# A transformer layer on one core: attention with its gate chunks and branch B in an order fixed by the text on all engines, tanh gates, and bias and mask summed behind the first FFN's down product

## The chip, the cores and the metric

The kernel runs on one core of a Trainium2 chip. A core has TensorE (PE: matmuls and transposes, results in PSUM banks of 128 x 512 floats), VectorE (DVE), ScalarE (ACT), GpSimd (POOL) and SyncE (SP, which here only starts DMAs; POOL starts some too). Each of them has a queue of its own. The metric is the device time of one execution in microseconds (us); less is better.

## The reference

One layer of an encoder, in float32, for 1024 tokens of width 1024:

```python
h = h + 0.5 * swiglu(rms_norm(h), w_gate, w_up, w_down)             # first FFN, 2816 wide
u = rms_norm(h)
qa, ka, va, qb, kb, vb, ga, gb = split(u @ w_in)
ya = neighbourhood_attention_2d(qa, ka, va, na_rpb)                 # branch A: 8 heads, relative bias and mask
yb = windowed_gqa_sink(rope(qb), rope(kb), vb, sink_logit)          # branch B: 8 heads on 2 kv heads, window, sink
merged = sigmoid(ga) * (ya @ w_branch_a) + sigmoid(gb) * (yb @ w_branch_b)
h = h + merged @ w_out
h = h + 0.5 * swiglu(rms_norm(h), ...)                              # second FFN
y = rms_norm(h)
```

Heads are 64 wide. In both attentions a block of 128 queries sees at most its own block of keys and its two neighbours.

## The kernel before

**Products.** Float32 operands are split into a high part (a copy on ACT in float32r) and a residual (source minus high part, DVE): `split`, L92 to L94. `mm3` (L142 to L149) makes a product of three matmuls for two banks: high times high, high times low, low times high. In each, the first operand is loaded as weights and serves both banks. Large products run by Strassen's scheme with seven sub-products P1 to P7 (`products`, L234; `Down`, L503). `Down.run` takes 77 steps for the FFN's down product (seven sub-products by 11 blocks of 128) and at each step calls the functions that are filed under its number in `loads`.

**Stages.** First FFN, hidden part and down product; the mixer's projection (five groups of four of the 34 column blocks of `w_in` that it needs); attention; branch products; output projection; second FFN. The other 14 column blocks are gate columns. They are not computed with the projection but as filling in attention (`gate`, L1132): a gate is a 128 x 1024 block, made in 48 matmuls of 128 x 512 into two PSUM banks; then ACT copies the banks out (L1143), and a DMA on POOL's queue stores them. Its weight is loaded as 128 x 1024 and split by one ACT cast (L93) and one DVE residual (L94).

**Attention** is 64 units, one for two heads and 128 queries: 32 of branch B (0 to 31), then 32 of branch A (32 to 63). Three steps, each a unit behind the one before: `scores` (L1284): for each head two matmuls of up to 128 x 384 (L1294, L1295), one DVE operation that adds bias or mask and finds the row's extreme (L1299), and the exp on ACT with its row sum (L1302); then reciprocal (L1305) and scaling, one head on DVE (L1306), one on ACT (L1307). `turn` (L1309): six transposes (L1315), with a split of each head (L93 on ACT, L94 on DVE). `values` (L1322): six matmuls (L1329 or L1334), a copy on ACT (L1247, L1268), and adds on DVE (L1249; L1269 and L1272). In the loop (L1352 to L1379) a turn has the scores of unit n, filling, the transposes of unit n - 1, filling, the values of unit n - 2. I call these the unit's first and second filling. Filling comes from the generator `filler` (L1215): the gates, then the products of branch B (`branch_b`, L1198) and of branch A.

**PSUM.** There are eight banks in two groups of four, g and d. Scores and transposes take d. Values and gates take g, a gate two banks at a time.

**Order.** Before, the text hands instructions to a scheduler, which decides each engine's order. Sigmoid opens the gates (L1195, L1409). The sum of bias and mask is made in `load_bias` (L1085 to L1091), two heads at a time, within attention.

## Time and profile before

| | |
|---|---|
| time, median of three runs | 1931.56 us (1931.3 to 1931.82) |
| the profiled execution | 1931.21 us, span 1929.4 us, clock 0.999 |
| busy: PE, DVE, ACT, POOL | 1919.3, 1434.0, 944.2, 296.1 us |
| first FFN: hidden part, down product | 0 to 413, 413 to 655 us |
| mixer's projection | 655 to 839 us |
| attention with gates | 839 to 1118 us |
| first branch products | 1118 to 1200 us |

A line of the profile's timeline has start, duration, engine, line, operation, and output<-input. Matmuls overlap and their ends are modelled, so a chain of them is read from start to start. A row of `order`, below, has the line, the operation, output<-input with the tiles' numbers, and the shape; [waits ...] names the engines whose semaphores the instruction waits for.

### The profile page before, as it was taken

The page shows a single profiled execution, that of the slowest core. Times are in us where ns is not written, and L with a number is a line of the kernel's source. Part 1 is how long each engine was busy: PE and PEld are TensorE (multiplying, and loading weights), DVE is VectorE, ACT ScalarE, POOL GpSimd, SP SyncE. Part 2 cuts the span into 40 slices and gives each one's busy share as a digit, 9 for nine tenths or more (in the row PEclk, how much of TensorE's full clock was granted, in tenths as well). Part 3 has the DMA queues.
Part 4 walks back from the last instruction along what each step waited for, and adds up shares of the span by engine and source line. Part 5 has one row for each costly group of instructions (what it writes and reads, how often), then busy time and mean ns, then how long its engine had stood idle before and what let it go on. Part 6 is the DMA issues. An engine that isn't in the chain of part 4 may idle for free.

```text
span 1929.4 us, 25478 instructions
## 1 busy us (share of the span) xinstructions
PE 1919.3 (99%) x8956; PEld 1602.7 (83%) x8956; DVE 1434.0 (74%) x2560; ACT 944.2 (49%) x1826; POOL 296.1 (15%) x432
## 2 busy tenths in 40 slices
PE   9999999999999999999999999999999999999998
PEld 8888888888888888888888888888888888888886
DVE  8987765668957778678888856889676566569864
ACT  7532333344446543477777862365333333344453
POOL 0011100013300112211122231010111001005210
PEclk9999999999999999999999999999999999999999
DMA  6244323285334467753459676443422322493341
GB/s 267 95 167 166 138 100 125 87 298 215 92 106 138 158 202 240 218 166 102 116 130 195 188 240 212 170 153 121 147 98 103 127 87 106 145 340 114 115 142 61
DMA packets 151745, 298.70 MB, mean 155 GB/s; under 512 B 14912, under 2 KB 64448, under 8 KB 151616
## 3 DMA queue, kind: packets, MB, share of 16 engines
q1 hardware_dynamic: 123072, 210.53, 33.3%
q0 software_dynamic: 27824, 85.48, 13.3%
q8 instruction: 71, 1.16, 0.2%
q10 hardware_dynamic: 720, 1.05, 0.1%
q14 instruction: 58, 0.48, 0.1%
HBM read 210.50 MB, written 88.27 MB: 155 GB/s over the span
## 4 chain that ended last, share of the span: by engine, by line
PE 96%; DVE 2%; ACT 1%; DMA 0%; issue 0%; POOLq 0%; POOL 0%; DVEq 0%
PE g L145 18%; PE g L147 18%; PE g L149 18%; PE d L149 12%; PE d L145 12%; PE d L147 12%; PE d L1315 2%; PE g L1329 1%; PE d L1294 1%; PE d L1295 1%; PE g L1334 1%; PE d L138 1%; DVE ar L94 0%; DMA ahead<-in_w_in_dram 0%; DMA n1c<-in_ffn_norm_dram 0%
## 5 line engine op out<-in xcount | busy, mean ns | idle before, releaser
L145 PE MATMUL g<-ar,ws 128*128 128x512 f32 x1128 | 422.6, 395 | 0.3 <-DVE fa L602 0.3
L147 PE MATMUL g<-ar,ws 128*128 128x512 f32 x1128 | 416.7, 390 | 0.0
L149 PE MATMUL g<-ar,ws 128*128 128x512 f32 x1128 | 416.3, 390 | 0.0
L145 PE MATMUL d<-ar,ws 128*128 128x512 f32 x736 | 281.9, 390 | 0.5 <-ACT ws L309 0.5
L147 PE MATMUL d<-ar,ws 128*128 128x512 f32 x736 | 281.4, 389 | 0.1
L149 PE MATMUL d<-ar,ws 128*128 128x512 f32 x736 | 281.2, 389 | 0.1
L149 PEld LDWEIGHTS g<-ar,ws 128*128 128x128 f32 x1128 | 211.7, 188 | 44.8
L147 PEld LDWEIGHTS g<-ar,ws 128*128 128x128 f32 x1128 | 211.8, 188 | 44.6
L145 PEld LDWEIGHTS g<-ar,ws 128*128 128x128 f32 x1128 | 206.4, 188 | 36.4 <-issue 0.7
L312 DVE TENSOR_TENSOR ws<-raw,ws 128x512 fp32r<-128x512 f32 x204 | 139.3, 689 | 98.9 <-ACT ws L309 97.9
L309 ACT CAST ws<-raw 128x512 fp32r<-128x512 f32 x204 | 125.0, 620 | 142.2 <-PE g L149 63.8
L145 PEld LDWEIGHTS d<-ar,ws 128*128 128x128 f32 x736 | 138.1, 188 | 29.4 <-ACT ws L309 0.9
L147 PEld LDWEIGHTS d<-ar,ws 128*128 128x128 f32 x736 | 138.1, 188 | 29.3 <-DVE ar L814 0.5
L149 PEld LDWEIGHTS d<-ar,ws 128*128 128x128 f32 x736 | 138.1, 188 | 29.1 <-DVE ws L312 0.5
L93 ACT CAST ws<-raw 128x512 fp32r<-128x512 f32 (+1 forms) x121 | 81.0, 669 | 144.7 <-PE d L149 66.7
L94 DVE TENSOR_TENSOR ws<-raw,ws 128x512 fp32r<-128x512 f32 (+1 forms) x119 | 94.0, 792 | 60.7 <-ACT ws L93 60.5
L415 POOL DMA_DIRECT2D hid<-fx x91 | 49.3, 542 | 432.3 <-DVE fx L475 288.6
L93 ACT CAST ar<-raw 128x512 fp32r<-128x512 f32 (+1 forms) x83 | 56.0, 679 | 93.7 <-PE g L147 55.0
L94 DVE TENSOR_TENSOR ws<-ar,ws 128x512 fp32r<-128x512 f32 x114 | 98.2, 866 | 4.0 <-ACT ws L93 3.9
L145 PE MATMUL g<-ws,ws 128*128 128x512 f32 x232 | 90.9, 392 | 0.0
L149 PE MATMUL g<-ws,ws 128*128 128x512 f32 x232 | 90.4, 390 | 0.0
L147 PE MATMUL g<-ws,ws 128*128 128x512 f32 x232 | 90.3, 389 | 0.0
(313 smaller groups left out, 3604.8 us busy)
## 6 DMA issues: line engine op xcount, KB each, us to landing
raw<-hid SPq DMA_DIRECT2D x70, 512.0 KB
hid<-fx POOLq DMA_DIRECT2D x91, 256.0 KB, 2.3
ar<-in_ffn_w_down_dram SPq DMA_DIRECT2D x32, 512.0 KB
raw<-in_ffn_w_up_dram SPq DMA_DIRECT2D x31, 512.0 KB
raw<-in_ffn_w_gate_dram SPq DMA_DIRECT2D x27, 512.0 KB
raw<-in_w_in_dram SPq DMA_DIRECT2D x27, 512.0 KB
hid<-fa POOLq DMA_DIRECT2D x51, 256.0 KB, 2.6
ar<-zs_d POOLq DMA_DIRECT2D x48, 256.0 KB, 5.0
```

The source lines that it names most:

```text
L93: nc.scalar.copy(dst_hi, src)
L94: (eng or nc.vector).tensor_tensor(dst_lo, src, f32v(dst_hi), op=ALU.subtract)
L138: nc.tensor.transpose(pt[:, c * P:(c + 1) * P], xs[:, (half * 4 + c) * P:(half * 4 + c + 1) * P], ident)
L145: nc.tensor.matmul(b, lhs[0], r[0], start=first, stop=False, **kw)
L147: nc.tensor.matmul(b, lhs[0], r[1], start=False, stop=False, **kw)
L149: nc.tensor.matmul(b, lhs[1], r[0], start=False, stop=last, **kw)
L309: nc.scalar.copy(w[0][:, :512], a)
L312: nc.vector.tensor_tensor(w[0][:, 512:], a, f32v(w[0][:, :512]), op=ALU.subtract)
L415: nc.gpsimd.dma_start(hid[PRODUCTS.index(p), i], src)
L1294: nc.tensor.matmul(b[:, :nw], un["q"][s], un["kd"][s][:, k0 * P:k1 * P], start=True, stop=False)
L1295: nc.tensor.matmul(b[:, :nw], un["q"][s], un["kl"][s][:, k0 * P:k1 * P], start=False, stop=True)
L1315: nc.tensor.transpose(pt[:, i * P:(i + 1) * P], un["pr"][s][:, i * P:(i + 1) * P], ident)
```

## The change

Attention runs in a manual schedule: each engine's queue follows the text. The text is rearranged for it. A unit's `scaled` comes behind the transposes of the unit before, so reciprocal and scaling stand behind that unit's casts and residuals. `values` returns the rest of its `write` as a generator, and DVE's add of the values' halves comes behind the scores of the next unit. `mm3_halves` lets a step of six matmuls be cut into two of three; a gate is 16 such steps, one and two a filling on even units, two and two on odd ones, so that a gate takes 4.57 units. Its weight is split five steps of six before its end, about a unit ahead of the next gate (in units 3, 8, 12, 17 and so on), as one cast of 128 x 1024 and one residual. The copies of the old gate stand where the filling generator reaches them. Gates end in units 4, 9, 13, 18, 22, 27, 31, 36, 41, 45, 50, 54, 59 and 63. The sinks of two heads are copied in one instruction; in branch B one 64 x 256 add replaces two of 64 x 128.

Sums of bias and mask are made in the first FFN's down product: in three calls for each of the eight heads, at steps 2, 5 and 10 plus six times the head's number, a load, two DVE adds, and two stores on SP's queue to `bm_d`. Attention loads the sums into six held tiles. Gates become tanh(x/2) + 1, multiplied in one fused DVE instruction, with the output projection's scale 0.5 in place of 1. Two of the mixer's early weight loads go to tiles that are free sooner, and are issued at the transition's first steps. The splits of y on POOL become splits on DVE, in units 59, 60 and 62 and in the last gate and branch B. The program has as many matmuls as before.

ACT around the end of a gate. Before: `xs_785` is the gate's copy, `g_733` and `g_734` its banks, `ws_765` the next gate's weight.

```order
L93 CAST ws_765_6870<-raw_767_6872 128x1024
L1307 ACTIVATE fa_73<-fa_73,rc_758_6834 128x384
L1247 COPY s1_692_6541<-g_768_6882 64x256
L1302 ACTIVATE fa_73,ssum_771_6894<-fa_73,nmx_770_6893 128x385 x2
L93 CAST ws_775_6917<-d_777_6919 128x3x128
L1307 ACTIVATE fa_73<-fa_73,rc_772_6895 128x384
L93 CAST ws_775_6917<-d_778_6925 128x3x128
L1143 COPY xs_785_6965<-g_733_6719 128x512
L1247 COPY s1_692_6541<-g_779_6937 64x256
L1143 COPY xs_785_6965<-g_734_6720 128x512
```

After, in units 12 and 13: `xs_859` is the copy, `g_809` and `g_810` the banks, `ws_847` the next weight.

```order
L1412 ACTIVATE fa_73<-fa_73,rc_840_7194 128x384
L98 CAST ws_847_7230<-raw_815_7076 128x1024
L1345 COPY s1_699_6593<-g_849_7237 64x256
L1402 ACTIVATE fa_73,ssum_851_7246<-fa_73,nmx_850_7245 128x385 x2
L98 CAST ws_855_7266<-d_857_7268 128x3x128
L98 CAST ws_855_7266<-d_858_7274 128x3x128
L1412 ACTIVATE fa_73<-fa_73,rc_852_7247 128x384
L1204 COPY xs_859_7286<-g_809_7051 128x512
L1204 COPY xs_859_7286<-g_810_7052 128x512
L1345 COPY s1_699_6593<-g_862_7295 64x256
```

The first copy stood behind the second cast of its unit, one copy of values after it; now both stand together, behind both casts and the scaling.

PE at the same two places. Before: the old gate's last matmuls, values (L1334), scores (L1294), then the new gate `g_786`, `g_787`.

```order
L149 MATMUL g_733_6719<-ar_439_4446,ws_710_6623 128x512
L149 MATMUL g_734_6720<-ar_76_589,ws_710_6623 128x512
L1334 MATMUL g_779_6937<-ws_761_6856,fx_649_6140 128x256
L1334 MATMUL g_779_6937<-ws_762_6857,fx_649_6140 128x256
...
L1294 MATMUL d_783_6950<-ar_478_4810,ar_479_4811 128x384 [waits DVE_49]
L1295 MATMUL d_783_6950<-ar_478_4810,ar_479_4811 128x384
L1294 MATMUL d_784_6956<-ar_478_4810,ar_479_4811 128x384 [waits DVE_49]
L1295 MATMUL d_784_6956<-ar_478_4810,ar_479_4811 128x384
L145 MATMUL g_786_6969<-ar_440_4447,ws_765_6870 128x512 [waits Activation_49]
L145 MATMUL g_787_6970<-ar_480_4812,ws_765_6870 128x512 [waits Activation_49]
```

After, unit 13 and the start of 14: the old gate's last three, the new gate `g_860`, `g_861`, values (L1439), scores (L1396).

```order
L162 MATMUL g_810_7052<-ar_76_590,ws_796_6991 128x512
L162 MATMUL g_809_7051<-ar_445_4495,ws_797_6992 128x512
L162 MATMUL g_810_7052<-ar_76_590,ws_797_6992 128x512
L162 MATMUL g_860_7290<-ar_446_4496,ws_847_7230 128x512 [waits Activation_49]
L162 MATMUL g_861_7291<-ar_493_4875,ws_847_7230 128x512 [waits DVE_49]
L162 MATMUL g_860_7290<-ar_446_4496,ws_847_7230 128x512
L1439 MATMUL g_862_7295<-ws_843_7210,fx_659_6195 128x256 [waits Activation_49]
L1439 MATMUL g_862_7295<-ws_844_7211,fx_659_6195 128x256
...
L1396 MATMUL d_866_7307<-ar_491_4873,ar_492_4874 128x384
L1397 MATMUL d_866_7307<-ar_491_4873,ar_492_4874 128x384
```

Before, the new gate began ten matmuls behind the old one's last. Now it follows at once, and the value product that waits for ACT comes three matmuls behind the old gate's last.

DVE at the weight's residual. Before: reciprocal, sink copy, scaling, the residual `ws_766`, the values' adds, then the reductions of the next unit (L1299).

```order
L1305 RECIPROCAL rc_758_6834<-ssum_757_6833 128x2
L1298 COPY fa_73<-nsk_5307 128x1
L1306 TENSOR_SCALAR fa_73<-fa_73,rc_758_6834 128x384
L94 TENSOR_TENSOR ws_766_6871<-raw_767_6872,ws_765_6870 128x1024
L1249 TENSOR_TENSOR xs_769_6889<-g_768_6882,s1_692_6541 64x128 x2
L1299 ISA fa_73,nmx_770_6893<-d_773_6896,masks_548_5302,nsk_5307 128x384
L1299 ISA nmx_770_6893 128x1
L1299 ISA fa_73,nmx_770_6893<-d_774_6902,masks_548_5302,nsk_5307 128x384
L1299 ISA nmx_770_6893 128x1
```

After, from unit 12's reciprocal to unit 13's residuals: `ws_848` is the weight's residual.

```order
L1410 RECIPROCAL rc_840_7194<-ssum_839_7193 128x2
L1411 TENSOR_SCALAR fa_73<-fa_73,rc_840_7194 128x384
L101 TENSOR_TENSOR ws_848_7231<-raw_815_7076,ws_847_7230 128x1024
L1393 COPY fa_73<-nsk_5361 128x2
L1399 ISA fa_73,nmx_850_7245<-d_853_7249,masks_557_5357,nsk_5361 128x384
L1399 ISA nmx_850_7245 128x1
L1399 ISA fa_73,nmx_850_7245<-d_854_7254,masks_557_5357,nsk_5361 128x384
L1399 ISA nmx_850_7245 128x1
L1347 TENSOR_TENSOR xs_827_7138<-g_849_7237,s1_699_6593 64x256
L101 TENSOR_TENSOR ws_856_7267<-d_857_7268,ws_855_7266 128x3x128
```

The residual stands ahead of the next unit's reductions in both; the add came before the reductions and comes now behind them, and the reciprocal is now behind the unit's own two residuals.

The core of the diff:

```diff
+    def mm3_halves(banks, first, last, lhs, rhs):
+
+        parts = [(w, b, r[k], k) for w, k in ((0, 0), (0, 1), (1, 0)) for b, r in zip(banks, rhs)]
+        for i, (w, b, r, k) in enumerate(parts):
+            nc.tensor.matmul(b, lhs[w], r, start=first and w + k == 0, stop=last and w == 1)
+            if i == 2:
+                yield
...
+                if i in early_rooms or (i, m) in early_rooms:
+                    ahead[i, m] = [main.tile([P, 512], F32, tag="hs", bufs=6, name=nm_("ahead")) for _ in range(2)]
+                    for k, r in enumerate(ahead[i, m]):
+                        nc.sync.dma_start(r.rearrange("p (c f) -> p c f", f=P), src(i, m, 0)[:, 4 * k:4 * k + 4])
+                else:
+                    ahead[i, m] = main.tile([P, 1024], F32, tag="ws", bufs=8, name=nm_("ahead"))
+                    fetch(ahead[i, m], i, m, 0)
...
+    bm_d = dram.tile([8, 2, P, 384], F32, name="bm_d")
+    biased = {}
+
+    def hs6():
+        return [main.tile([P, 512], F32, tag="hs", bufs=6, name=nm_("hs"))[:, :384] for _ in range(6)]
+
+    def bias_fetch(h):
+        if h == 0:
+            biased[0] = hs6()
+            for e in range(2):
+                nc.sync.dma_start(biased[0][e], c_mask_a[e])
+        nc.sync.dma_start(biased[0][2 + h % 2], bias_d[h])
+
+    def bias_add(h):
+        for e in range(2):
+            o = biased[0][4 + e]
+            pin(nc.vector.tensor_tensor(o.rearrange("p (d r w) -> p d r w", d=3, r=ROWS),
+                                        biased[0][2 + h % 2].rearrange("p (r d w) -> p d r w", d=3, w=8),
+                                        biased[0][e].rearrange("p (d r w) -> p d r w", d=3, r=ROWS), op=ALU.add))
+
+    def bias_put(h):
+        for e in range(2):
+            nc.sync.dma_start(bm_d[h, e], biased[0][4 + e])
+
+    for h in range(8):
+        for e, f in ((2, bias_fetch), (5, bias_add), (10, bias_put)):
+            k = e + 6 * h
+            down.loads.setdefault(k, []).insert(0, lambda d, f=f, h=h: f(h))
...
+    def gate_split(late=False):
+        h, l, r = ws4(), ws4(), mix["gate"]
+        split(h, l, r, None, late)
+        mix["gate"] = [a.rearrange("p (c f) -> p c f", f=P) for a in (h, l)]
...
-            mm3(bs, k == 0, k == NC8 - 1, (w[0][:, c, :], w[1][:, c, :]), [u_half(c, n) for n in range(2)])
-            yield
+            yield from mm3_halves(bs, k == 0, k == NC8 - 1, (w[0][:, c, :], w[1][:, c, :]), [u_half(c, n) for n in range(2)])
+            if k < NC8 - 1:
+                yield
             if k in steps:
...
+    def open_gate(dc):
+        r = mix["rb", dc]
+        pin(nc.scalar.activation(r, r, AF.Tanh, scale=0.5))
...
-                nc.vector.tensor_tensor(merged(dc)[:, sl], bs[n], rb[:, sl], op=ALU.mult)
+                nc.vector.scalar_tensor_tensor(out=merged(dc)[:, sl], in0=rb[:, sl], scalar=1.0, in1=bs[n],
+                                               op0=ALU.add, op1=ALU.mult)
...
-                yield from gate(dc, {4: lambda: mix.update(gate=load_w(win[0], GA + nxt * P))})
+                yield from gate(dc, {0: lambda: gate_fetch(nxt, raw4()), 5: gate_split})
             else:
-                yield from gate(dc, {0: lambda: [fetch_y(c * P) for c in range(2)],
-                                     4: lambda: [split_y(Y_B[c], c * P, nc.gpsimd) for c in range(2)],
-                                     5: lambda: [fetch_y(c * P) for c in range(2, 4)]})
+                yield from gate(dc, {0: lambda: [fetch_w(0), fetch_w(1)] + [fetch_y(c * P) for c in range(2)],
+                                     2: lambda: fetch_gate(0),
+                                     4: lambda: [split_y(Y_B[0], 0, nc.vector), fetch_y(2 * P)],
+                                     5: lambda: split_w(0),
+                                     6: lambda: [split_y(Y_B[1], P, nc.vector), fetch_y(3 * P)]})
...
                     nc.scalar.copy(lo, o[HD:])
+                    yield
-                    for s in range(2):
-                        nc.vector.tensor_tensor(ybox["b"][s * HD:s * HD + HD, c, :], o[:HD, s, :], lo[:, s, :], op=ALU.add)
+                    yield
+                    nc.vector.tensor_tensor(ybox["b"][:, c], o[:HD], lo, op=ALU.add)
...
+        un["sums"] = ssum, rc
+
+    def scaled(un):
+
+        ssum, rc = un["sums"]
         nc.vector.reciprocal(rc, ssum)
         nc.vector.tensor_scalar_mul(un["pr"][0], un["pr"][0], rc[:, 0:1])
         nc.scalar.activation(un["pr"][1], un["pr"][1], AF.Copy, scale=rc[:, 1:2])
...
-        un["write"](o)
+        rest = un["write"](o)
+        next(rest)
+        return rest
...
-    rate = (nfill - 44) / 64.0
-    spent = 3.0
-
-    def filling(share):
+    n_b = 64
+    spent = 0.0
+
+    def filling(n):
         nonlocal spent
-        spent += rate * share
+        spent += len(gates) * 8 / n_b if n < n_b else 2
         drain(fill, int(spent))
         spent -= int(spent)
...
-    for n in range(1 << 30):
-        got = next(source, None)
-        if got is not None:
-            scores(got)
-        pipe.insert(0, got)
-        for hp, n0 in preps.items():
-            if n == n0:
-                prep = prep_a(hp)
-        if prep:
-            drain(prep, 1)
-        filling(0.5)
-        if len(pipe) > 1 and pipe[1] is not None:
-            turn(pipe[1])
-        if prep:
-            drain(prep, 1)
-        if n in (58, 59, 61):
-            fetch_y(512 + min(n - 58, 2) * P)
-        if n in (60, 61, 62):
-            split_y(Y_A[n - 60], 512 + (n - 60) * P, nc.gpsimd)
-        filling(0.5)
-        if len(pipe) > 2 and pipe[2] is not None:
-            values(pipe[2])
-        pipe = pipe[:3]
-        if not any(pipe):
-            break
-    drain(fill)
+    def attention():
+
+        nonlocal pipe, prep
+        rest = iter(())
+        for n in range(1 << 30):
+            got = next(source, None)
+            if got is not None:
+                scores(got)
+            drain(rest)
+            pipe.insert(0, got)
+            for hp, n0 in preps.items():
+                if n == n0:
+                    prep = prep_a(hp)
+            if prep:
+                drain(prep, 1)
+            filling(n)
+            if len(pipe) > 1 and pipe[1] is not None:
+                turn(pipe[1])
+            if got is not None:
+                scaled(got)
+            if prep:
+                drain(prep, 1)
+            if n >= 26 and (n - 26) % 8 == 0 and n < 58:
+                fetch_bias((n - 26) // 8)
+            if n in (56, 57, 59):
+                fetch_y(512 + min(n - 56, 2) * P)
+            if n in (59, 60, 62):
+                split_y(Y_A[min(n - 59, 2)], 512 + min(n - 59, 2) * P, nc.vector)
+            filling(n)
+            if len(pipe) > 2 and pipe[2] is not None:
+                rest = values(pipe[2])
+            pipe = pipe[:3]
+            if not any(pipe):
+                break
+        drain(rest)
+        drain(fill)
+
+    by_text[0] = True
+    with tc.manual_schedule(engines={E.DVE, E.Activation, E.PE, E.SP, E.Pool}):
+        attention()
+    by_text[0] = False
...
-    down = Down(4, wo[0], 1.0, place, quarter, {k: left_d[i] for i, k in enumerate(("P5", "P6", "P3", "P7"))},
+    down = Down(4, wo[0], 0.5, place, quarter, {k: left_d[i] for i, k in enumerate(("P5", "P6", "P3", "P7"))},
...
-            nc.vector.tensor_tensor(r[:, sl], bs[n], r[:, sl], op=ALU.mult)
+            nc.vector.scalar_tensor_tensor(out=r[:, sl], in0=r[:, sl], scalar=1.0, in1=bs[n], op0=ALU.add, op1=ALU.mult)
```

More of the change, by code (lines that the diff above doesn't have):

```diff
@@ L394, in post @@
                 drain(run, 10)
-            if t in (3, 4):
-                load_ahead(t - 2)
+            for i, n in zip((1, 2), sooner or (3, 4)):
+                if t == n:
+                    load_ahead(i)
         return post
@@ L939, in down1 @@
         return res(t)
-    pin = tc.keep_in_program_order
     def rope_load(k):
@@ L1215, in filler, with a_open @@
+    def a_open(i):
+        r = mix["ra", i]
+        pin(nc.scalar.activation(r, r, AF.Tanh, scale=0.5))
     def filler():
@@ L1255, in units_b @@
                            kd=[kd_b()[g]] * 2, kl=[kl_b()[g]] * 2, v=[mix["vb"][g]], bias=[mask_b] * 2,
-                           sink=[nsk[:, 2 * c + s:2 * c + s + 1] for s in range(2)], write=write)
+                           sink=nsk[:, 2 * c:2 * c + 2], write=write)
     def units_a():
@@ L1279, in units_a @@
                 yield dict(j=j, q=[qs[s][:, tj] for s in range(2)], kd=kd, kl=kl, v=va,
-                           bias=[bias_slot(s)[:, edge, :] for s in range(2)], sink=None, write=write)
+                           bias=[bias_at(hp, s, edge) for s in range(2)], sink=None, write=write)
     npair = [0]
```

183 lines of the change are left out of this document (106 added, 77 removed).

## The prediction

> **What bounds the kernel now.** I read the page's engine list and chain first, then the waits of TensorE (PE), then busy time by stage.
>
> ```profile
> PE 1919.3 (99%) x8956; PEld 1602.7 (83%) x8956; DVE 1434.0 (74%) x2560; ACT 944.2 (49%) x1826; POOL 296.1 (15%) x432
> PE 96%; DVE 2%; ACT 1%; DMA 0%; issue 0%; POOLq 0%; POOL 0%; DVEq 0%
> PE g L733 <- POOL ident masks.py:199: 1.5, 1, 1.5
> PE d L145 <- ACT ws L309: 0.5, 1, 0.5
> PE d L1315 <- DVE ws L94: 0.3, 1, 0.3
> PE g L145 <- DVE fa L602: 0.3, 1, 0.3
> 413.00:655.00 242.00, 241.73 (x1090) 199.90 (x1089) 181.60 (x246) 113.80 (x204) 46.33 (x43) 1.00 0.47 159
> 655.00:839.00 184.00, 183.53 (x822) 151.81 (x821) 145.57 (x219) 87.52 (x155) 33.25 (x61) 1.00 0.67 205
> 839.00:980.00 141.00, 140.52 (x822) 122.67 (x820) 116.18 (x396) 110.95 (x280) 21.55 (x37) 1.00 0.45 126
> 980.00:1118.00 138.00, 137.99 (x822) 121.71 (x823) 120.19 (x381) 114.87 (x295) 33.72 (x45) 1.00 0.66 171
> 1118.00:1200.00 82.00, 82.00 (x367) 67.78 (x366) 46.40 (x74) 36.66 (x48) 18.62 (x20) 1.00 0.72 244
> ```
>
> Line one is PE, weight load, VectorE (DVE), ScalarE (ACT), GpSimd; line two the chain of work that ended last. Then come all of PE's waits in the list (total, times, longest), and the stages: length, then PE, weight load, DVE, ACT, POOL busy, clock, DMA. PE does 99% of the span; the change keeps its matmuls, so nothing big can be won. In the two attention rows (839 to 1118) PE shows 0.5 us idle, but DVE is 82% and 87% busy and ACT 79% and 83%. There a fixed order can lose time: each of these queues runs in its order, and one late instruction delays all behind it.
>
> **Durations for the sum.** Three timelines of before around a gate's end (start, duration, and what runs):
>
> ```profile
> 870.68 0.82 PE L1315 MATMUL d<-ident,fa 128*128 128x128 f32 x6
> 872.26 0.62 PE L149 MATMUL g<-ar,ws 128*128 128x512 f32 x2
> 872.72 0.87 PE L1334 MATMUL g<-ws,fx 128*128 128x256 f32 x6
> 873.43 0.34 PE L1294 MATMUL d<-ar,ar 128*128 128x384 f32 x1
> 873.61 0.34 PE L1295 MATMUL d<-ar,ar 128*128 128x384 f32 x1
> 874.13 0.81 PE L145 MATMUL g<-ar,ws 128*128 128x512 f32 x2
> ```
> ```profile
> 867.72 1.05 ACT L93 CAST ws<-raw 128x1024 fp32r<-128x1024 f32 x1
> 868.65 0.62 ACT L1307 ACTIVATE fa<-fa,rc 128x384 f32<-128x384 f32 x1
> ...
> 871.21 0.62 ACT L1302 ACTIVATE fa<-fa,nmx 128x385 f32<-128x385 f32 x1 [1.53 <-DVE nmx L1299]
> ...
> 871.82 0.60 ACT L1302 ACTIVATE fa<-fa,nmx 128x385 f32<-128x385 f32 x1
> ...
> 872.54 0.48 ACT L93 CAST ws<-d 128x384 fp32r<-128x384 f32 x1
> 872.91 0.62 ACT L1307 ACTIVATE fa<-fa,rc 128x384 f32<-128x384 f32 x1
> 873.43 0.47 ACT L93 CAST ws<-d 128x384 fp32r<-128x384 f32 x1
> 873.79 0.60 ACT L1143 COPY xs<-g 128x512 f32<-128x512 f32 x1
> 874.41 0.37 ACT L1247 COPY s<-g 64x256 f32<-64x256 f32 x1
> ```
> ```profile
> 866.87 1.02 DVE L94 TENSOR_TENSOR ws<-d,ws 128x384 fp32r<-128x384 f32 x2
> 867.86 0.17 DVE L1305 RECIPROCAL rc<-ssum 128x2 f32<-128x2 f32 x1
> 867.94 0.13 DVE L1298 COPY fa<-nsk 128x1 f32<-128x1 f32 x1
> 868.06 0.42 DVE L1306 TENSOR_SCALAR fa<-fa,rc 128x384 f32<-128x384 f32 x1
> 868.79 1.23 DVE L94 TENSOR_TENSOR ws<-raw,ws 128x1024 fp32r<-128x1024 f32 x1 [0.31 <-ACT ws L93]
> 869.94 0.57 DVE L1249 TENSOR_TENSOR xs<-g,s 64x128 f32<-64x128 f32 x2
> 870.54 0.62 DVE L1299 CUSTOM_DVE_ANT_0 fa<-d,masks,nsk 128x384 f32<-128x384 f32 x1
> ```
>
> A queue goes on before a result is out, so I read the step from start to start: 128x512 matmul 0.23 (872.26 to 872.72 for two), 128x384 0.17, the six value matmuls 0.71, six transposes 0.65; on ACT exp 0.61, cast 0.37, scale 0.52, gate copy 0.48 (result 0.60), weight cast 0.93; on DVE reduction 0.55, residual 0.46, reciprocal 0.09, scale 0.33, weight residual 1.13. Between engines lies little (cast's end 868.77, residual's start 868.79); I take 0.04. A 64x256 add is taken as 0.33 (the pair of 64x128 takes 0.57).
>
> **Cost of the gate ends.** In after, a unit on PE is scores 0.70, filling 0.68 or 1.36, transposes 0.65, filling 1.36, values 0.71: 4.10 or 4.78 us, 4.44 on average. DVE needs 2 x 0.55 + 0.33 + 2 x 0.46 + 0.09 + 0.33 + 0.10 = 2.87 and ACT 2 x 0.61 + 2 x 0.37 + 0.52 + 0.28 = 2.76, so a plain unit waits for nothing. A gate's end doesn't fit. Group g has four PSUM banks: two for the gate, two for values. There the new gate takes the value banks (its second matmul needs DVE's add of this unit), and the next value product needs the old gate's first bank, copied out by ACT. In before that copy stands right behind the second cast (873.79) and six value and four score matmuls stand between the old gate and the new: PE loses 0.19 (874.13, two matmuls in 0.81 instead of 0.62). In after the copy stands behind the scale of the same unit, which needs the reciprocal, which DVE does only behind the add and both residuals; and PE runs the value product two matmuls after the new gate began.
>
> Unit 13, from its start: the weight cast of unit 12 runs 0.50 to 1.55, its residual on DVE 1.59 to 2.72, sink copy to 2.82. Reductions start at 2.82 and 3.37 instead of about 0.55; add result 4.33. PE: scores to 0.70, gate to 2.06, transposes to 2.71, last three of the old gate to 3.39, new gate's first to 3.61; its second should start at 3.61 and waits to 4.36: **0.75**. Exps 3.48 to 4.70, casts to 5.44, residuals 5.22 to 6.14, reciprocal result 6.31, scale 6.35 to 6.87, copy result 7.46. The values should start at 4.82 and wait to 7.50: **2.68**. Without the weight residual the reductions start at 0.55, but the casts wait for the transposes, the scale starts at 4.24 and the copy's result is out at 5.35, 1.3 behind the values at 4.07. So two causes: the order alone costs 1.3, the weight split ahead of the next reductions 2.1 more. Behind the waiting value product stand the scores of unit 14, for which DVE and ACT wait in turn; PE has no slack elsewhere, so what it loses here is not given back.
>
> The same addition for each gate end (with the split / without): units 4, 13, 36, 45, with the copy in the second filling: 3.3/1.8, 3.4/1.3, 3.5/1.9, 3.5/1.8. Units 9, 18, 27, 41, 50, with it in the first: 1.9/0.5, 0.6/0, 2.0/0.4, 1.3/0.3, 0.5/0. Units 22, 31, 54, where a gate ends with a unit's filling: 2.0/0.2, 1.3/0, 2.3/0.2. Sum 25.6/8.4. The A half uses its own row for the reduction, 0.07 shorter:
>
> ```profile
> L1299 DVE CUSTOM_DVE_ANT_0 fa<-d,fa 128x384 f32<-128x384 f32 x20 | 10.9, 549 | 3.0 <-PE d L1295 2.8
> ```
>
> At units 59 to 66 the last gate end meets seven 128x1024 splits of y, 1.13 each on DVE, one or two ahead of the next reductions, and the first branch products, whose weight and y halves they are: 10.6/8.5. Total **36.2** (17 without the split's delay).
>
> **The rest.** What before loses at gate ends goes: thirteen times 0.19 is 2.5, minus 2.5. Sixteen bias-and-mask adds of 0.55 leave attention for the FFN 1 down product, where DVE is idle 60 of 242 us: 0, bounds minus 0.3 (all that PE idles there) and plus 1.5 (the longest wait in the list). The bound above is for SP: its stores of the sums wait for the add, and weight fetches queue behind them. They come five of 77 steps after it, about 16 us (242 / 77 x 5), so the wait should be over. Earlier loads for the mixer: PE idles 0.47 of 184, so minus 0.5 to plus 1.5, value 0. Tanh for sigmoid, and the fused add and multiply in DVE: as many instructions as before, ACT and DVE idle 45 and 36 of 82 us there, PE 82.00 busy: 0, and still 0 if all of them together took 30 us longer. The table load that goes lies there too: 0.
>
> The sum is 1931.2 (the profiled execution, 0.3 below the median) + 36.2 - 2.5 = **1964.9**, say 1965.
>
> **Rivals.**
> (1) Only the bank waits remain, because the split is absorbed: 1931.2 + 17 - 2.5 = **1946**. For it: in before the same residual (868.79) holds the reductions to 870.54, two microseconds behind their scores, and PE runs on. Against it: there reciprocal and scale stand ahead of residuals and between casts; in after they are last.
> (2) The waits are long enough to close PE's clock. Slices after PE's last work, at 1922.3, (length, busy, clock, DMA):
>
> ```profile
> 1922.00:1923.00 1.00, 0.29 (x2) 0.00 (x0) 0.73 (x2) 0.04 (x1) 0.00 (x0) 1.00 0.05 20
> 1925.00:1926.00 1.00, 0.00 (x0) 0.00 (x0) 0.47 (x1) 0.43 (x1) 0.00 (x0) 0.77 0.00 0
> 1926.00:1927.00 1.00, 0.00 (x0) 0.00 (x0) 0.00 (x0) 0.00 (x0) 0.00 (x0) 0.50 0.67 256
> ```
>
> The clock falls at about 1925.5, 3.3 us after PE went idle. The value waits of units 36 and 45 are 3.3, four others 2.3 to 2.7. If six waits cost a stretch of 3.3 at half clock, each adds 1.6: 10; if all thirteen, 21: **1975 to 1986**. Against: most waits are shorter than 3.3. The Trainium skill, "TensorE: Matmul & The Clock Gate", section "What's actually happening", has the clock at half after an idle window of about 3.4 us, counted free-running. By that rule a shorter wait never fills a window, and this case adds nothing; the end of this trace agrees with 3.3, and no row of before has such a wait in mid-program.
> (3) The other side: the copies come in time, and only before's 2.5 goes: **1929**. It takes place at unit 13's value product and its twelve like. The price is all of the 36; it decides if the copy's result is out before the values can start, which is 1.3 us (without split) or 2.7 us (with) sooner than I add up. For it: the steps come from a handful of rows, and I may have one dependence too many. Against: the same addition along before's own order, from 863.7 to 875, meets the trace within 0.05 us, with one miss of 0.3; 1.3 is more than that.
> (4) The change doesn't do what it says, or something hidden undoes the waits: within 1929 to 1934, almost excluded, since the order is printed.
>
> **Chances.** Forecast 0.60 (own range 1955 to 1974); (1) 0.17 (1942 to 1952); (2) 0.13; (3) 0.08; (4) 0.02. A measurement of this kernel can tell about 0.2% (3.9 us) from no change: faster 0.05 (the better half of 3), same 0.05, slower 0.90. The range 1942 to 1980 takes in the forecast, (1) and half of (2), with the bounds of 1.5 and 1.5; some 0.17 is left out.
>
> **What would show it.** In after's waits of PE: values (L1439) waiting for ACT's gate copy (L1204), about seven times, 2 to 3.5 us each, and the gate's second matmul (L162) waiting for DVE's add (L1347, L1369), 0.3 to 1.9; DVE's reductions starting over 2 us behind their scores in units 13, 22 and their like; PE idle around 8 us over units 59 to 66; no wait over 0.5 in FFN 1 down. If PE waits for DMA in attention, if units 5 to 7 (plain) wait, or if the waits at gate ends are under 1 us, I am wrong. Clock under 1.00 in attention would speak for (2).

## The result and the profile after

The changed kernel takes 1989.1 us (median of four runs, 1987.39 to 1990.48) against 1931.69: 1.0297 times as long, with an interval of 1.028 to 1.0313. The forecast was 1965, with a range of 1942 to 1980: the right side, but 24 us too little, and outside the range.

The engines and the chain of work that ended last, then TensorE's (PE's) waits, of the changed kernel:

```profile
PE 1940.0 (98%) x8956; PEld 1611.8 (81%) x8956; DVE 1434.4 (72%) x2505; ACT 947.2 (48%) x1826; POOL 282.0 (14%) x424
PE 87%; DVE 6%; ACT 5%; issue 1%; DMA 0%; SPq 0%; POOLq 0%; DVEq 0%; ACTq 0%; POOL 0%
```
```profile
PE g L162 <- ACT xs L1204: 6.2, 3, 2.8
PE g L1434 <- ACT xs L1204: 6.2, 2, 3.1
PE g L1439 <- ACT xs L1204: 5.5, 3, 2.6
PE g L162 <- DVE fa L1369: 5.1, 4, 1.9
PE g L162 <- DVE xs L1347: 4.9, 4, 2.0
PE d L1420 <- DVE fa L1411: 3.4, 4, 1.7
PE d L1420 <- DVE nmx L1399: 2.8, 2, 1.6
```

PE's busy time grew by 21 us although it runs the same 8956 matmuls: some of them ran slower (14.9 us, below), and some 5 us are modelled ends ahead of waits (see the note on counting). The waits are those that were named: values (L1434 in branch A, L1439 in branch B) and gate matmuls (L162) for ACT's gate copy, gate matmuls for DVE's add. The stages show where all of it lies (length; PE, weight load, DVE, ACT, POOL busy; clock; DMA):

```profile
413.00:655.00 242.00, 241.98 (x1091) 200.35 (x1090) 188.03 (x266) 116.08 (x209) 52.47 (x44) 1.00 0.53 180
655.00:839.00 184.00, 183.95 (x823) 151.86 (x822) 145.35 (x217) 87.88 (x152) 32.42 (x59) 1.00 0.68 207
839.00:980.00 141.00, 128.26 (x703) 110.11 (x701) 89.22 (x275) 93.85 (x232) 14.43 (x25) 0.95 0.37 96
980.00:1118.00 138.00, 123.24 (x689) 105.34 (x690) 94.13 (x301) 93.32 (x244) 25.71 (x48) 0.96 0.67 161
1118.00:1200.00 82.00, 71.81 (x362) 58.75 (x361) 56.85 (x148) 53.63 (x116) 2.69 (x5) 0.96 0.42 148
```

Up to 839 us nothing is lost. From 839 to 1200 PE idles 37.7 us, and its clock, 1.00 up to there and in the kernel before, is 0.95 to 0.96 on the mean. DVE and ACT are less busy than they were in attention: no engine took over as the bound.

### The profile page after: what moved, and what is told of

Read it like the earlier page. It is cut to its first block, busy times and chain, and to the rows that moved or that the text cites. A ratio compares the mean times of both kernels' runs of the same rounds, so it can differ in the third digit from the quotient of the medians.

```text
span 1987.3 us, 25595 instructions
## 1 busy us (share of the span) xinstructions
PE 1940.0 (98%) x8956; PEld 1611.8 (81%) x8956; DVE 1434.4 (72%) x2505; ACT 947.2 (48%) x1826; POOL 282.0 (14%) x424
## 3 DMA queue, kind: packets, MB, share of 16 engines
q10 hardware_dynamic: 720, 1.05, 0.1%
## 4 chain that ended last, share of the span: by engine, by line
PE 87%; DVE 6%; ACT 5%; issue 1%; DMA 0%; SPq 0%; POOLq 0%; DVEq 0%; ACTq 0%; POOL 0%
PE g L152 14%; PE g L156 14%; PE g L154 14%; PE d L156 11%; PE d L152 11%; PE d L154 11%; PE g L162 6%; DVE ws L101 2%; PE d L162 2%; ACT fa L1402 2%; ACT ws L98 1%; PE d L1420 1%; DVE fa L1399 1%; DVE ar L101 1%; PE g L1439 1%
## 5 line engine op out<-in xcount | busy, mean ns | idle before, releaser
L152 PE MATMUL g<-ar,ws 128*128 128x512 f32 x840 | 327.4, 390 | 0.0
L156 PE MATMUL g<-ar,ws 128*128 128x512 f32 x840 | 326.8, 389 | 0.0
L154 PE MATMUL g<-ar,ws 128*128 128x512 f32 x840 | 326.8, 389 | 0.0
L152 PE MATMUL d<-ar,ws 128*128 128x512 f32 x672 | 262.4, 391 | 0.2 <-ACT ar L863 0.2
L154 PE MATMUL d<-ar,ws 128*128 128x512 f32 x672 | 261.7, 389 | 0.6 <-DVE ar L865 0.6
L156 PE MATMUL d<-ar,ws 128*128 128x512 f32 x672 | 261.6, 389 | 0.1
L162 PE MATMUL g<-ar,ws 128*128 128x512 f32 x864 | 238.3, 412 | 16.2 <-ACT xs L1204 6.2
L162 PEld LDWEIGHTS g<-ar,ws 128*128 128x128 f32 x864 | 160.9, 195 | 47.3 <-ACT xs L1204 7.2
L154 PEld LDWEIGHTS d<-ar,ws 128*128 128x128 f32 x672 | 126.2, 188 | 27.2 <-DVE ar L865 1.2
L152 PEld LDWEIGHTS d<-ar,ws 128*128 128x128 f32 x672 | 126.1, 188 | 27.0 <-ACT ar L863 0.7
L156 PEld LDWEIGHTS d<-ar,ws 128*128 128x128 f32 x672 | 126.1, 188 | 26.7 <-DVE ws L333 0.7
L98 ACT CAST ws<-raw 128x512 fp32r<-128x512 f32 (+1 forms) x111 | 74.5, 671 | 133.8 <-PE d L156 63.7
L101 DVE TENSOR_TENSOR ws<-raw,ws 128x512 fp32r<-128x512 f32 (+1 forms) x111 | 88.9, 801 | 63.3 <-ACT ws L98 63.1
L101 DVE TENSOR_TENSOR ws<-d,ws 128x384 fp32r<-128x384 f32 (+1 forms) x128 | 61.4, 519 | 50.5 <-ACT ws L98 50.3
```

What stands on the lines that cost most here:

```text
L98: hi = nc.scalar.copy(dst_hi, src)
L101: (eng or nc.vector).tensor_tensor(dst_lo, src, f32v(dst_hi), op=ALU.subtract)
L152: nc.tensor.matmul(b, lhs[0], r[0], start=first, stop=False, **kw)
L154: nc.tensor.matmul(b, lhs[0], r[1], start=False, stop=False, **kw)
L156: nc.tensor.matmul(b, lhs[1], r[0], start=False, stop=last, **kw)
L162: nc.tensor.matmul(b, lhs[w], r, start=first and w + k == 0, stop=last and w == 1)
```

## The experiments

A note on counting. A wait is shown from the modelled end of the matmul ahead, 0.39 after its start, though the next could have started 0.23 after it; so each wait costs some 0.16 more than the list has. I count waits from start to start in the timeline, less the plain step: 43.5 us in the changed kernel for 34 waits from 839 us on. Stretches at half clock are counted from the clock's record.

| run | edit on the changed kernel | us | to before | waits | stretches at half clock |
|---|---|---|---|---|---|
| changed kernel | | 1989.1 | 1.0297 [1.028, 1.0313] | 43.5 | 9 |
| split_pool | weight residuals on GpSimd | 1972.48 | 1.0206 [1.019, 1.0222] | 32.2 | 4 |
| scale_last | scaling behind the second filling | 1962.18 | 1.0153 [1.0138, 1.0168] | 27.7 | 2 |
| both_moves | both | 1953.02 | 1.0108 [1.0093, 1.0123] | 20.2 | 2 |
| busy_waits2 | idle PE kept busy | 1977.15 | 1.0233 [1.0218, 1.0248] | 25.8 | 2 |
| gap | empty step behind each gate | 1974.62 | 1.022 [1.0202, 1.0237] | 35.7 | 6 |
| gap_moves | empty step and both moves | 1953.9 | 1.0113 [1.0098, 1.0128] | 21.0 | 2 |
| y_pool | y's residuals on GpSimd | 1989.55 | 1.0298 [1.0282, 1.0313] | 40.5 | 14 |
| text_best | four moves | 2025.51 | 1.0482 [1.0465, 1.05] | 76.7 | 12 |
| scheduled | order left to the scheduler | 1936.52 | 1.0019 [1.0009, 1.0029] | 4.1 | 2 |
| sched_y_later | the same, third split of y later | 1938.14 | 1.003 [1.0019, 1.0041] | 6.4 | 1 |
| sched_y_pool | the same, splits of y as before | 1934.59 | 1.0014 [1.0004, 1.0024] | 4.2 | 0 |

### Is it the fixed order? (scheduled)

```diff
-    by_text[0] = True
-    with tc.manual_schedule(engines={E.DVE, E.Activation, E.PE, E.SP, E.Pool}):
-        attention()
-    by_text[0] = False
+    attention()
```

> Edit: attention is handed to the scheduler again (no manual schedule); the text and all other parts of the change stay. Theory A (only the fixed order costs): 1929 to 1935 us, no wait over 1 us in attention. Rival E (the sums behind the first FFN's down product, tanh, the splits of y on VectorE or the early loads cost something): over 1940 us, with waits at the branch products or in the first FFN.

1936.52 us: 52.6 of the 57.4 go with the manual schedule alone; the sums behind the FFN, tanh, the early loads and the new text stay. The time is 1.5 above what was expected, and rival E has a small part of it: 4 to 5 us are left (3.7 by the ratio, 4.8 by the medians). They lie at one place, where the last unit's transposes wait for the scaling on ACT:

```profile
1121.33 0.99 PE L1434 MATMUL g<-ws,fx 128*128 128x256 f32 x6
1122.49 0.41 PE L1420 MATMUL d<-ident,fa 128*128 128x128 f32 x2 [0.17 <-DVE fa L1411]
1124.94 0.69 PE L1420 MATMUL d<-ident,fa 128*128 128x128 f32 x2 [2.04 <-ACT fa L1412]
```
```profile
1123.43 1.04 ACT L98 CAST ar<-raw 128x1024 fp32r<-128x1024 f32 x1 [1.80 <-DMA raw<-y_d]
1124.38 0.50 ACT L1412 ACTIVATE fa<-fa,rc 128x256 f32<-128x256 f32 x1
```

On ACT the cast of a y stands ahead of the scaling and waits 1.80 us for its DMA. The two stretches at half clock, from 1124.84 to 1131.66, lie right behind this wait. Two runs followed this end.

### The end, with the scheduler (sched_y_later, sched_y_pool)

sched_y_later splits the third y in unit 63 in place of 62.

```diff
-            if n in (59, 60, 62):
+            if n in (59, 60, 63):
```

> Edit: attention handed to the scheduler, and the third split of y from the A half in unit 63 in place of 62 (its cast on ScalarE waited 1.8 us for its DMA, ahead of the scaling that the last unit's transposes needed). Theory A: the 2.2 us wait and the two stretches at half clock behind it go, 5 us in all: 1930 to 1933 us, level with before. Rival H (the end of attention is late for another reason, such as the weights' splits): 1935 to 1938 us.

1938.14: no gain. The 2.04 us wait is gone, but the first branch product now waits 4.1 us for another y. Rival H's time came out within 0.2 us, though the weights' splits aren't the reason. The expectation took the cast at 1123.43 of scheduled for the A half's third y; by the layout that it writes, it is one of branch B's, and the A half's third was cast at 1115.48. In sched_y_later that third y's residual ends only at 1124.05 (1117.79 in scheduled). The load of branch B's last y, which that residual releases, is issued at 1124.08 (the `raw` tiles of the loads have four buffers); its cast waits 4.14 us for this DMA, and the product waits for the cast. sched_y_pool puts these splits where before had them:

```diff
-                split_y(Y_A[min(n - 59, 2)], 512 + min(n - 59, 2) * P, nc.vector)
+                split_y(Y_A[n - 60], 512 + (n - 60) * P, nc.gpsimd)
...
-                                     4: lambda: [split_y(Y_B[0], 0, nc.vector), fetch_y(2 * P)],
+                                     4: lambda: [split_y(Y_B[0], 0, nc.gpsimd), fetch_y(2 * P)],
```

> Edit: attention handed to the scheduler, the splits of y from branches A and B with their residuals on GpSimd and in the units of before (60, 61, 62; loads in 58, 59, 61). Theory A (what is left of the loss with the scheduler lies in these splits alone): no wait over 1 us at the end of attention, 1930 to 1934 us. Rival H (the branch weights' place or their splits make the end late): 1935 to 1940 us.

1934.59, 0.6 above what was expected, with no half clock, but with waits of 1.08 and 1.39 us at the first branch products, so not quite as theory A had it. All but 2.7 us of the change is then accounted for.

### The two causes at a gate's end (split_pool, scale_last, both_moves)

```diff
-        split(h, l, r, None, late)
+        split(h, l, r, nc.gpsimd if late is None else None, late)
...
-                yield from gate(dc, {0: lambda: gate_fetch(nxt, raw4()), 5: gate_split})
+                yield from gate(dc, {0: lambda: gate_fetch(nxt, raw4()), 5: lambda: gate_split(None)})
```

> Edit: the residual of the gates' weights is made on GpSimd in place of VectorE; nothing else. Theory A (the loss has three sources: the weight's residual holds up VectorE's reductions, the gate's copies stand behind the scaling on ScalarE, and TensorE's clock is halved for 3.4 us after a stretch of 3.4 us in which it idled about 1.9 us or more): the value products of units 4, 13, 36 and 45 still wait, but 1.7 to 1.9 us each instead of 2.4 to 3.3; all waits in attention fall from 43 to about 24 us; half clock in at most 3 stretches instead of 8; 1953 to 1962 us. Rival B (the residual is absorbed, the copies' place alone matters): waits stay near 43, 1980 to 1990 us.

1972.48: between A and B. The residual's delay is real (11 us of waits and 5 stretches less), but the value waits fell less than I added up: units 4, 13, 36 and 45 still wait 2.3, 2.0, 2.8 and 3.4.

```diff
-            if got is not None:
-                scaled(got)
...
             filling(n)
+            if got is not None:
+                scaled(got)
             if len(pipe) > 2 and pipe[2] is not None:
```

> Edit: reciprocal and scaling of a unit are written behind its second filling, so the gate's copies and weight cast stand ahead of the scaling on ScalarE; nothing else. Theory A: the value products of units 4, 13, 45 wait about 0.9 us instead of 2.4 to 3.3, that of 36 about 2.3; all waits fall from 43 to 20 to 24 us; half clock in at most 3 stretches; 1951 to 1962 us. Rival C (the weight's residual alone matters): value waits shrink by less than 0.5 each, 1978 to 1990 us.

1962.18, 0.2 above the upper end of A. The value waits are 1.1 in unit 4, 1.3 in 13, 1.0 in 27, 2.0 in 36 and 1.9 in 45, and only two stretches at half clock are left. So the scaling's place ahead of the copies is the larger cause: 26.9 us for moving one block of text, against 16.6 for the residual. But this edit mends a part of the residual's delay too, for the weight's cast also comes ahead of the scaling: for unit 13, DVE's first reduction starts 1.7 us behind the last score matmul (898.33 to 900.01), where it was 2.6 in the changed kernel (903.23 to 905.83). How much of the 26.9 us is the copies' alone wasn't measured.

> Edit: the weights' residuals on GpSimd and the scaling behind the second filling, together. Theory A: the two causes add up; waits in attention fall from 43.5 (32 and 28 with one edit alone) to 14 to 18 us, no stretch at half clock but perhaps one: 1943 to 1950 us. Rival F (both edits mend the same waits): no better than the scaling alone, 1958 to 1963 us.

1953.02. Better than either, so F falls, but 36 us in place of the 43.5 that the two gains add up to, and above A's 1950. The causes overlap, as that reduction shows. Its largest waits:

```profile
PE d L1420 <- DVE fa L1411: 4.2, 5, 2.3
PE g L162 <- DVE xs L1347: 3.1, 3, 2.0
PE g L162 <- DVE fa L1369: 3.0, 2, 2.2
PE g L1434 <- ACT xs L1204: 2.4, 2, 1.3
PE g L1439 <- ACT xs L1204: 2.1, 3, 1.1
```

### The clock (busy_waits2, probe)

Unit 13's two waits in the changed kernel, PE, and then five stretches of the clock's grid (columns as in the stages):

```profile
905.37 1.17 PE L162 MATMUL g<-ar,ws 128*128 128x512 f32 x4
907.38 0.73 PE L162 MATMUL g<-ar,ws 128*128 128x512 f32 x2 [0.84 <-DVE xs L1347]
910.66 1.44 PE L1439 MATMUL g<-ws,fx 128*128 128x256 f32 x5 [2.55 <-ACT xs L1204]
```
```profile
902.97:906.38 3.41, 3.41 (x20) 2.74 (x18) 2.04 (x6) 1.75 (x3) 0.00 (x0) 1.00 0.00 0
906.38:909.80 3.42, 0.89 (x3) 0.30 (x2) 2.37 (x10) 2.44 (x7) 0.00 (x0) 1.00 0.87 311
909.80:913.21 3.41, 2.55 (x10) 2.55 (x11) 0.38 (x3) 1.67 (x4) 0.55 (x1) 0.50 0.41 158
913.21:916.62 3.41, 3.41 (x13) 2.92 (x12) 1.92 (x6) 2.26 (x6) 0.72 (x1) 0.50 0.34 102
916.62:920.04 3.42, 3.42 (x20) 3.04 (x20) 2.26 (x9) 1.50 (x4) 0.00 (x0) 1.00 0.23 43
```

The clock changes only on a grid of 3.41 us: in each trace of these runs, all its changes lie within 0.002 us of one grid of 3.413 us. PE was busy 0.89 in the second stretch, and the next two run at 0.50. busy_waits2 adds 72 matmuls, 16 us of work, in the idle time (a first form of it, busy_waits, gave no time):

```diff
+            for _ in range(again if i == 0 else 0):
+                nc.tensor.matmul(b, lhs[w], r, start=True, stop=True)
...
+            if n in (4, 13, 36, 45):
+                b, h = bank("d"), u_half(4, 0)[0]
+                for _ in range(10):
+                    nc.tensor.matmul(b, h[:, :P], h, start=True, stop=True)
```

`again` is 8 for the first step of the gates that begin in units 9, 22, 41 and 54.

> Edit: work that is not used fills the long waits of TensorE: eight more matmuls ahead of the gate's first one in the gates that begin in units 9, 22, 41 and 54 (1.8 us each, overwritten), ten into an idle bank ahead of the value products of units 4, 13, 36 and 45 (2.3 us each). 72 matmuls more, 16.4 us of TensorE work; the result stays the same. Theory A (clock): the waits' ends stay, so the added work costs under 2 us, and all but one or two of the 9 stretches at half clock go, 1.7 us each: 1974 to 1979 us, faster than with less work. Rival D (the clock costs nothing): 1988 to 1994 us; if the work isn't hidden at all, 2005.

1977.15: with more work the kernel is 12 us faster, as A had it, and 7 of the 9 stretches are gone. The same place:

```profile
904.83 2.45 PE L1496 MATMUL d<-ar 128*128 128x512 f32 x10
907.56 0.98 PE L1442 MATMUL g<-ws,fx 128*128 128x256 f32 x6 [0.28 <-ACT xs L1207]
```

The filling takes 2.45 us, nothing but 0.28 of waiting is left behind it, and the matmuls that follow run at full clock. D falls. The probe then looked for the threshold:

```diff
+            if n == 2:
+                b, u = bank("d"), u_half(4, 0)[0]
...
+                for copies in (2, 3, 4, 5, 6, 7) * 4:
+                    for _ in range(copies):
+                        nc.scalar.copy(x, b)
+                    for r in [x] + 36 * [u]:
+                        nc.tensor.matmul(b, u[:, :P], r, start=True, stop=True)
```

> The changed kernel with a probe of the clock at the start of unit 2, in the order of the text: 24 times, ScalarE makes 2, 3, 4, 5, 6 or 7 copies of 128x512 out of a bank, a matmul waits for them (estimated at 1.3, 1.8, 2.3, 2.7, 3.2 and 3.7 us of idle TensorE, four times each, at whatever point of the clock's 3.41 us grid they fall), then 36 matmuls of 128x512 follow (8.2 us). The probe's work isn't part of the computation. Theory A: the clock is halved for one stretch of the grid exactly when TensorE idled about 2 us or more within the stretch before; never after 1.3 and 1.8, after 2.3 and 2.7 only when they lie mostly in one stretch. Some 8 to 14 of the 24 waits are followed by half clock; about 2255 to 2275 us. Rival I (the clock is halved only after a stretch without any matmul, 3.41 us): none after waits up to 3.2, at most a few after 3.7.

2296.07 us, in a single run. A copy of this kind takes 0.61, so the waits are 1.5, 2.1, 2.7, 3.4, 4.0 and 4.6 us, longer than expected, and so is the time. Two waits of the probe, each with three stretches of the grid:

```profile
937.37 0.50 PE L1475 MATMUL d<-xs,ar 128*128 128x512 f32 x1 [1.96 <-ACT xs L1473]
```
```profile
932.16:935.57 3.41, 3.25 (x15) 2.35 (x13) 0.00 (x0) 0.07 (x1) 0.00 (x0) 1.00 0.00 0
935.57:938.98 3.41, 1.61 (x7) 1.35 (x8) 0.00 (x0) 1.68 (x3) 0.00 (x0) 1.00 0.02 5
938.99:942.40 3.41, 3.41 (x17) 2.81 (x16) 0.00 (x0) 0.00 (x0) 0.00 (x0) 1.00 0.00 0
880.96:884.37 3.41, 2.08 (x10) 1.38 (x8) 0.00 (x0) 1.18 (x3) 0.00 (x0) 1.00 0.00 0
884.38:887.78 3.40, 1.54 (x7) 1.28 (x8) 0.00 (x0) 1.74 (x3) 0.00 (x0) 1.00 0.00 0
887.79:891.20 3.41, 3.41 (x10) 2.65 (x9) 0.00 (x0) 0.00 (x0) 0.00 (x0) 0.50 0.02 5
```

1.61 us busy in a stretch keeps the clock, 1.54 does not. Over the probe's waits, every stretch at full clock with up to 1.80 us of idle PE was followed by full clock, and every one with 1.86 or more by half. Of the 24 waits 15 were followed by half clock, one more than expected: none of those of 1.5 and 2.1 us but the very first, which took 2.5, two of the four of 2.7, and all longer ones. Rival I falls.

### The hand-over of banks (gap, gap_moves)

```diff
         nc.gpsimd.dma_start(g_d[dc * P:(dc + 1) * P, :], gt)
         yield
+        yield
...
-        spent += len(gates) * 8 / n_b if n < n_b else 2
+        spent += len(gates) * 8.5 / n_b if n < n_b else 2
```

> Edit: an empty step of filling behind each gate's copies, so that the new gate never follows the old one's end at once (238 steps in place of 224, and the rate of filling is raised to suit); nothing else. Theory A (the site of the loss is the hand-over of banks: the new gate takes the banks of the values, and values then wait for the gate's copy): most waits of values for the copy and of the gate's second matmul for the add go, though not in units where gate and values still meet in one filling (4 and 13); waits 12 to 22 us in all, at most 4 stretches at half clock; 1942 to 1958 us. Rival K (the queues of VectorE and ScalarE are late by themselves, the banks only show it): waits stay over 30 us, above 1970 us.

1974.62, with 35.7 us of waits: A missed, and both of K's numbers came out. Values wait only 2.4 us in all for the copy (6.2 + 5.5 in the changed kernel), as A had it, but gate matmuls now wait 7.0 us for the copy and transposes 7.2 for DVE's scaling. Most of the loss moved on along the same chain, as K had it: the queues are late, and the banks are one place where it shows.

> Edit: the empty step of the run before, the weights' residuals on GpSimd and the scaling behind the second filling, together; order fixed by the text. Theory A: nothing of the gate ends is left but some tenths each, and the end of attention (4 to 8 us); 1937 to 1946 us. Rival K (something in the fixed order costs besides gate ends and the end): over 1948 us.

1953.9, level with both_moves (1953.02). With copies and residual moved, the empty step brings nothing; what is left there isn't the hand-over of banks to values. Rival K's time came out, but what the 21 us of waits have in common wasn't tried further.

### The end, with the fixed order (y_pool)

```diff
-                split_y(Y_A[min(n - 59, 2)], 512 + min(n - 59, 2) * P, nc.vector)
+                split_y(Y_A[min(n - 59, 2)], 512 + min(n - 59, 2) * P, nc.gpsimd)
...
-                        split_y(Y_B[3], 3 * P, nc.vector)
+                        split_y(Y_B[3], 3 * P, nc.gpsimd)
```

> Edit: the order fixed by the text as in the changed kernel, with six of the splits of y making their residual on GpSimd in place of VectorE; nothing else. Theory A: the waits of the transposes for VectorE in units 59 to 63 (1.2 and 1.9 us) and the half clock at 1165 shrink or go, the first products of the branches wait for GpSimd instead: 3 to 7 us less than the changed kernel, 1982 to 1986 us. Rival J (VectorE has room for these splits, ScalarE's casts and the weights set the end): 1987 to 1991 us.

1989.55, no gain, so J's time came out, though not for J's reason: waits fell by 3.0 us as A had it, and 14 stretches in place of 9 fell to half clock. Where a wait of a given length falls on the grid decides.

### Four moves at once (text_best)

```diff
                 rest = values(pipe[2])
+                drain(rest)
```

besides both moves, and the third split of y in unit 63.

> Edit: the order still fixed by the text, with four moves: residuals of the weights on GpSimd, scaling behind the second filling, the add of the values' halves ahead of the next reductions, the third split of y from the A half a unit later (63 in place of 62). Theory A: waits of the gate's second matmul for the add go, those at the end shrink: all waits 6 to 13 us, no half clock: 1935 to 1944 us. Rival G (banks are handed over too early in this order whatever the queues do): waits stay over 15 us, 1947 us or more.

2025.51, the slowest of all. A missed; G's bounds hold (76.7 us of waits), but the trace shows another reason than the one that G gives. Three adds and what lies between them, on DVE:

```profile
867.86 0.42 DVE L1347 TENSOR_TENSOR xs<-g,s 64x256 f32<-64x256 f32 x1 [0.68 <-ACT s L1345]
868.20 0.15 DVE L1393 COPY fa<-nsk 128x2 f32<-128x2 f32 x1
868.50 0.62 DVE L1399 CUSTOM_DVE_ANT_0 fa<-d,masks,nsk 128x384 f32<-128x384 f32 x1
...
871.94 0.16 DVE L1410 RECIPROCAL rc<-ssum 128x2 f32<-128x2 f32 x1
872.13 0.42 DVE L1411 TENSOR_SCALAR fa<-fa,rc 128x384 f32<-128x384 f32 x1
873.24 0.42 DVE L1347 TENSOR_TENSOR xs<-g,s 64x256 f32<-64x256 f32 x1 [0.68 <-ACT s L1345]
...
878.61 0.42 DVE L1347 TENSOR_TENSOR xs<-g,s 64x256 f32<-64x256 f32 x1 [0.68 <-ACT s L1345]
```

The add now stands ahead of the reductions and waits for ACT's copy of values; that copy stands behind ACT's scaling; the scaling needs the reciprocal, which comes behind residuals, casts, exps and reductions. That is a loop through both queues, once a unit: 5.38 us from add to add in most plain units of branch B, where PE has work for 4.44. Scaling last alone made no such loop: in both_moves the shortest plain units take 4.28.

## Why the prediction was wrong, point by point

**Side and place: right.** All of the loss lies from 839 to 1200 us. FFN 1 and the projection cost nothing, as the stages show, and what follows is shifted by 57.9 us.

**The waits' mechanism: right in the main.** In unit 13 the forecast was 0.75 for the add and 2.68 for the copy; 0.84 and 2.55 are shown, about 1.0 and 2.7 from start to start. scale_last and split_pool, one part of the cause each, both gain. Rival (1), the residual absorbed, falls with split_pool's 16.6 us. But the prediction had the loss as a wait for banks at the gates' ends, and gap shows that most of it stays when values hardly wait for them any more. Values waited for the copy five times, where about seven were forecast.

**The waits' size: 43.5 where the sum had 36.2.** At the twelve gate ends with a price of their own: 4.0, 2.2, 3.7, 0.9, 2.9, 3.3, 1.4, 4.2, 2.0, 4.6, 1.2 and 3.4 for units 4, 9, 13, 18, 22, 27, 31, 36, 41, 45, 50 and 54, together 33.8 where 25.6 was forecast. Unit 59 to the first branch products: about 9 (10.6). Part of the difference is a wait that the sum didn't have: transposes that wait until DVE's reduction is done (L1420 for L1399), 1.8 us in unit 27 and 1.3 in unit 45. This term's error alone would have given some 1972, inside the range. "A plain unit waits for nothing" held.

**The step that failed: that most waits are too short for the clock.** I set its cost at 0, took the 3.3 us that the clock took to fall at the end of before's trace for the length that a wait must have, and gave the rival 0.13. That end couldn't tell: counted back from the fall at 1925.54, its stretch of 3.41 us has 0.17 of work, so it fits any smaller threshold too. In fact some 1.9 us of idle within one stretch of 3.41 suffices. Nine stretches, 30.7 us, ran at half clock with PE idle for 0.9 of them: (30.7 - 0.9) / 2 = 14.9 us. busy_waits2 shows that this is a cost of its own, for the time fell by 12 while work was added. Rival (2) as worked out asked for waits near 3.3 and 1975 to 1986; its price for the clock, 10 to 21, came out with another condition. The clock's cost alone would have given some 1980, the edge of the range; it took both errors to leave it.

The Trainium skill, "TensorE: Matmul & The Clock Gate", section "What's actually happening", gives the free-running window of about 3.4 us, and the grid here agrees, at 3.41. Its condition, an idle window, does not hold here: the probe's 1.86 us of 3.41 is enough, and the measurement decides.

**The 2.5 us that before should lose at gate ends: not there.** I took the one gate start that I had read, at 874.13, thirteen times. The other twelve lose 0.05 at most beyond a plain step; the next new gate's first two matmuls take 0.63, not 0.81:

```profile
895.79 0.63 PE L145 MATMUL g<-ar,ws 128*128 128x512 f32 x2
```

By the count that gives 43.5, before waits 1.0 us in attention, at three other places. The account: 43.5 + 14.9 - 1.0 is 57.4, against 57.9 of span.

**The rest at nothing: nearly.** With the scheduler, the other parts cost 4 to 5 us, all at the end of attention, where I had 0. The splits of y in their new places are 1.9 of them (1936.52 less 1934.59), a difference no larger than the spread of scheduled's runs (1934.81 to 1937.03).

**Still open.** What causes the last 20 us of waits in both_moves, one by one; how much of the loss is the copies' alone; and why the value waits fell less in split_pool than added up. No version with the fixed order comes near before, and none with the scheduler beats it.

## What to carry to other kernels

Before an order is fixed by hand, walk each resource that changes hands (here four PSUM banks) and each pair of queues for a chain that leads back to its start; one instruction behind another queue's late result costs its delay at every turn. Price a wait of the matmul engine twice, once for its length and once for the clock that it may halve behind it; where a wait of 2 us can't be avoided, matmuls that nobody needs can be cheaper than idling, as they were in busy_waits2. And before one reading is multiplied, read a second place of the same kind.

## What the runs showed of the hardware

The clock is set stretch by stretch on a fixed grid of 3.41 us, by what PE did in the stretch before. At full clock, 1.80 us idle keep it and 1.86 halve it (probe). So a wait of 2.75 us that the grid cuts in two costs nothing more: unit 22 of the changed kernel, the wait and its stretches:

```profile
959.28 0.96 PE L162 MATMUL g<-ar,ws 128*128 128x512 f32 x3 [2.75 <-ACT xs L1204]
```
```profile
954.18:957.59 3.41, 2.34 (x14) 1.81 (x13) 2.25 (x9) 2.17 (x6) 0.73 (x1) 1.00 0.55 159
957.59:961.00 3.41, 1.72 (x10) 1.46 (x11) 2.53 (x9) 2.84 (x7) 0.99 (x2) 1.00 0.38 72
961.01:964.42 3.41, 3.41 (x22) 3.10 (x20) 2.18 (x8) 2.16 (x6) 3.41 (x8) 1.00 0.99 291
```

In attention itself, in the runs above, the line was less sharp: by the busy time that the stages' view shows, stretches with 1.4 to 1.9 us idle went both ways. Counted from start to start, as the waits are, the line was narrower in all runs: stretches with less than 1.98 us idle kept the clock (up to 1.93 in the probe), those with more than 2.17 halved it, and between the two both happened. At half clock less is enough to stay there: counted the same way, 0.94 us and more kept it halved (1.00 in the stretch from 909.80 above), and 0.69 and less did not (0.68 in busy_waits2).
